# Gather, running sum and projection: fp32 gathers with a ScalarE cast in place of converting gathers, and some stores in two transfers

## The chip, the cores and the metric

The kernel runs on one core of a Trainium2 chip. The time is that of the device in microseconds (us), from the start of one execution to its end. The profile shows one such execution; its span goes from the first to the last instruction on the core and is a little shorter than the time. Engines are named as the profile does: PE is TensorE, DVE is VectorE, ACT is ScalarE, POOL is GpSimd, SP is SyncE. Besides them 16 DMA engines move data between HBM and the on-chip memory.

## What is computed

```python
B, S, N, D = 16, 4096, 2048, 512
# x: fp32 [B, S, D]; indices: int64 [B, N], ascending, without repeats; w: fp32 [D, D]
gathered = x[arange(B)[:, None], indices, :]
cs = cumsum(gathered, axis=1)
out = matmul(cs, w)          # fp32 [B, N, D]
```

For each of 16 batches 2048 rows of 512 numbers are gathered, a running sum is taken over them, and each summed row is multiplied by a 512 x 512 matrix. 67.1 MB are read by the gathers and 67.1 MB are written.

## The kernel before

The rows are cut into 256 tiles of 128 (16 a batch, `NT`), and two tiles make a pair (`R = 2`, 128 pairs). There is no scheduler: each engine has its own list of instructions, written out in order, and waits on semaphores. `Lane.need` puts a wait in only where the engine has not yet waited for as much. A tile passes through these steps:

- `gather(t)`, POOL, L112: an indirect DMA fetches 128 rows of `x`, one per partition. The destination `g16` is fp16 and the source fp32, so the DMA converts. There are `NG = 16` tile buffers (eight pairs); before POOL issues a gather it waits (`s_a`) until PE has summed the pair that was in the buffer.
- `sums(t)`, PE, L130: four matmuls with `g16` as the stationary operand and a triangle of ones (`ut`, or `uq` in the first and last pair) as the moving one. The result `pa` is the running sum within the tile, transposed: the 512 columns lie on the partitions in four blocks. There are four `pa` buffers.
- `carry(t)`, DVE, L162 (L149 at the start of a batch): adds the last column of the tile before and writes fp16 to `cst`. Four pair buffers.
- `project(u)`, PE, L173: four matmuls of 128x128 by 128x512, summed into one bank `pb`; four banks. The matrix `w` was converted to `w16` at the start (ACT at L319, DVE at L290).
- `drain(u)`, ACT, L185: copies `pb` to the fp32 output buffer `ob`, eight pair buffers. Before the first drain of a pair ACT waits until the store that last read that buffer has landed.
- `store(g)`, SP, L199: one DMA of 128 partitions by 1024 numbers (4 KB a partition) per pair, when both drains are done. The first and the last pair are stored tile by tile (L194), and their rows lie in plain order (`PLAIN`); in the others the triangle `ut` interleaves the rows so that each partition holds two neighbouring output rows.

PE's order is made ahead of time: sums run in front of projections by a lead that grows from 1 to `LEAD = 4` tiles over the first tiles and falls again over the last ones:

```python
lead = min(LEAD, 1 + u // 8, 1 + (T - 1 - u) // 6)
first = u if u // R in PLAIN else u // R * R + R - 1
while done < T and done <= max(first, u + lead):
```

DVE takes the carries in order of tiles, ACT the drains, SP the stores, POOL the gathers. Before the loop small DMAs bring indices and weights, and PE runs some matmuls on zeros (L269) until the first tile is there.

Of the kernel before, what the change touches and what calls it, by code (L numbers as in the profile page):

```python
# [7 lines left out]
P = 128  # L8
FP32 = mybir.dt.float32
FP16 = mybir.dt.float16  # L10
# [17 lines left out]
def kernel(  # L28
# [7 lines left out]
    nc = tc.nc  # L36

    B, S, D = x.shape
    N = indices.shape[1]
    R = 2  # L40
# [3 lines left out]
    T = B * NT  # L44
    G = T // R
# [2 lines left out]
    FIRST = 2 * R  # L48
    NG = 16
    LEAD = 4  # L50
    NA = 4
    NB = 4
    NC = 4
    NO = 8
    assert D == 512 and N % (R * P) == 0 and T % P == 0

    x_flat = x.rearrange("b s d -> (b s) d")

    const = ctx.enter_context(tc.tile_pool(name="const", bufs=1))
# [10 lines left out]
    ident = const.tile([P, P], FP32)  # L70
    zeros = const.tile([P, D], FP16)
    spare = const.tile([P, 1], FP16)
    g16 = [const.tile([P, R, D], FP16, name=f"g16_{i}") for i in range(NG // R)]
    cst = [const.tile([P, DC, R, P], FP16, name=f"cst{i}") for i in range(NC)]
    ob = [const.tile([P, R, D], FP32, name=f"ob{i}") for i in range(NO)]
    pa = [ps.tile([P, DC, R, Q], FP32, name=f"pa{i}") for i in range(NA)]
    pb = [ps.tile([P, D], FP32, name=f"pb{i}") for i in range(NB)]
# [3 lines left out]
    def sem(name):  # L81
        return tc.alloc_semaphore(name)

    s_z, s_ut, s_wc, s_if, s_pt, s_prep, s_of, s_c = (
        sem(f"s_{n}") for n in ("z", "ut", "wc", "if", "pt", "prep", "of", "c")
    )
# [5 lines left out]
    s_g = [sem(f"s_g{i}") for i in range(NG)]  # L92
    s_o = [sem(f"s_o{i}") for i in range(NO)]
    s_a = sem("s_a")
    s_d = sem("s_d")
    s_b = sem("s_b")
    s_e = sem("s_e")

    pool, pe, dve, act, sp = (
        Lane(e) for e in (nc.gpsimd, nc.tensor, nc.vector, nc.scalar, nc.sync)  # L100
    )

    def gather(t):
        g, r = divmod(t, R)
        pool.need(s_a, R * (g + 1) - NG)
        if t < FIRST:
            pool.need(s_first[g], 16)
            ap = idx_first[:, t, 0:1]
        else:
            pool.need(s_prep, t // P + 1)  # L110
            ap = idxg[:, t // P, t % P : t % P + 1]
        nc.gpsimd.indirect_dma_start(  # L112
            out=g16[g % (NG // R)][:, r, :],
            out_offset=None,
            in_=x_flat,
            in_offset=bass.IndirectOffsetOnAxis(ap=ap, axis=0),
            element_offset=(t // NT) * S * D,
        ).then_inc(s_g[t % NG], 16)


    PLAIN = (0, G - 1)

    def sums(t, u):
        g, r = divmod(t, R)
        pe.need(s_g[t % NG], 16 * (t // NG + 1))
        pe.need(s_d, t - NA + 1)
        for c in range(DC):
            if c == 1 and u is not None:
                pe.need(s_e, u - NB + 1)
            mm = nc.tensor.matmul(  # L130
                out=pa[t % NA][:, c],
                lhsT=g16[g % (NG // R)][:, r, c * P : (c + 1) * P],
                rhs=uq[:] if g in PLAIN else ut[:],
                start=(c == 0),
                stop=(c == DC - 1),
            )
        mm.then_inc(s_a, 1)

    def carry(t):
        g, r = divmod(t, R)  # L140
        dve.need(s_a, t + 1)
        src = pa[t % NA][:]
        if g in PLAIN:
# [22 lines left out]
    def project(u, t):  # L166
# [3 lines left out]
        for c in range(DC):  # L170
            if c == 2 and t is not None:
                pe.need(s_d, t - NA + 1)
            mm = nc.tensor.matmul(  # L173
# [8 lines left out]
    def drain(u):  # L182
        g, j = divmod(u, R)
        act.need(s_b, u + 1)
        nc.scalar.copy(out=ob[g % NO][:, j], in_=pb[u % NB][:]).then_inc(s_e, 1)  # L185

    def store(g):
        b, h = divmod(g, GB)
        rows = out[b, h * R * P : (h + 1) * R * P, :]
        if g in PLAIN:  # L190
            for j in range(R):
                sp.need(s_e, R * g + j + 1)
                done = s_ol[j] if g else (s_o[0], s_of)[j]
                nc.sync.dma_start(  # L194
                    out=rows[j * P : (j + 1) * P, :], in_=ob[g % NO][:, j]
                ).then_inc(done, 16)
            return
        sp.need(s_e, R * (g + 1))
        nc.sync.dma_start(  # L199
            out=rows.rearrange("(p j) d -> p j d", j=R), in_=ob[g % NO][:]  # L200
        ).then_inc(s_o[g % NO], 16)


    with nc.allow_non_contiguous_dma(reason="a few indices, one per partition"):
        for k, eng in enumerate((nc.sync, nc.scalar)):
            t = k * R
            eng.dma_start(  # L207
                out=idx_first[:, t : t + R, :],
                in_=indices[0, t * P : (t + R) * P]
# [7 lines left out]
    for k in range(KI):  # L217
        nc.sync.dma_start(
            out=idx64[:, k, :], in_=idx_rows[k * P : (k + 1) * P, :]
        ).then_inc(s_idx[k], 16)  # L220
    for g in range(G):
        store(g)
    for g in range(G - NO, G - 1):
        sp.need(s_o[g % NO], 16 * (g // NO + 1))
    for j in range(R):
        sp.need(s_ol[j], 16)

# [5 lines left out]
        out=ident[:],  # L233
        in_=ident[:],
# [7 lines left out]
        out=ut[:],  # L242
        in_=ut[:],
# [9 lines left out]
        out=uq[:],  # L253
        in_=uq[:],
# [6 lines left out]
    for t in range(T):  # L261
        gather(t)
# [15 lines left out]
    for k in range(KI):  # L278
# [3 lines left out]
            out=pb[k % NB][:, :P], in_=idxf[:, k, :], identity=ident[:]  # L282
# [16 lines left out]
    for u in range(T):  # L299
        lead = min(LEAD, 1 + u // 8, 1 + (T - 1 - u) // 6)  # L300
        first = u if u // R in PLAIN else u // R * R + R - 1
# [4 lines left out]
    for i, (is_sums, t) in enumerate(order):  # L306
        after = next((v for k, v in order[i + 1 :] if k != is_sums), None)
        if is_sums:
            sums(t, after)
        else:  # L310
            pe.need(s_wc, DC)
            project(t, after)
# [7 lines left out]
    for u in range(T):  # L320
        if u % R == 0:
            if u == R * NO:
                act.need(s_of, 16)
            act.need(s_o[u // R % NO], 16 * (u // R // NO))
        drain(u)


# [28 lines left out]
```

## Time and profile before

| | |
|---|---|
| time, median of 3 runs (lowest to highest) | 356.53 us (356.07 to 357.17) |
| the profiled execution: time, span | 356.07 us, 354.4 us |
| granted TensorE clock, mean | 0.993 |
| PE busy, share of the span | 310.2 us, 88% |
| ACT busy | 152.7 us, 43% |
| DVE busy | 179.0 us, 51% |
| POOL busy | 242.1 us, 68% |
| DMA packets, data moved (counted where it lands) | 57018, 102.35 MB |
| HBM read, written | 68.42 MB, 67.11 MB |
| gathers: time from issue to landing, median | 14.7 us |
| stores of a pair: issue to landing, median | 6.2 us |

Busy time is added up over all instructions of an engine; matmuls are pipelined, so a busy PE is not PE at its peak. The DMA digits of the slices are the mean busy share of the 16 DMA engines. Queue q0 carries POOL's gathers, q1 what SP issues (the stores above all). "POOL" in the chain that ended last is the issue of gathers, "DMA" the time from an issue to its landing where that is what the next step waited for.

### The profile page before, as it was taken

To read this page: it belongs to the slowest core of one execution; us is meant where nothing else is said; L and a number is where in the kernel's file an instruction comes from. 1 tells how busy PE (TensorE), PEld (TensorE's weight loads), DVE (VectorE), ACT (ScalarE), POOL (GpSimd) and SP (SyncE) were. 2 spreads that over 40 slices of the span, in tenths; PEclk is the share of its full clock that TensorE was granted. 3 is DMA by queue.
4 is the path that set the end of the run, shared out by engine and by line. 5 is a ranking of instruction groups with operands and counts; after the bars stand their busy time and mean duration, and the time that the engine had idled before them with its cause. 6 is when DMAs were issued, how large, how long until landed. Compare 5 with 4: busy or idle time off the path is not lost.

```text
span 354.4 us, 5499 instructions
## 1 busy us (share of the span) xinstructions
PE 310.2 (88%) x2071; PEld 148.7 (42%) x2071; DVE 179.0 (51%) x263; ACT 152.7 (43%) x260; POOL 242.1 (68%) x266
## 2 busy tenths in 40 slices
PE   5879899898899899898998898988988998889984
PEld 2345344344444444444444343444434444344432
DVE  1356555454555455455554555554555555455441
ACT  2135344444444444444444444444444444444542
POOL 6777777777777777777777777777767776776000
PEclk9899999999999999999999999999999999999998
DMA  7899999999999999999999999999999999999995
GB/s 192 122 235 276 307 280 307 296 296 310 292 302 307 289 312 296 295 305 298 303 303 294 302 300 296 298 306 293 304 302 302 302 294 302 306 290 304 310 322 204
DMA packets 57018, 102.35 MB, mean 289 GB/s; under 512 B 6816, under 2 KB 39840, under 8 KB 56992
## 3 DMA queue, kind: packets, MB, share of 16 engines
q0 software_dynamic: 36864, 33.57, 58.1%
q1 hardware_dynamic: 19568, 67.91, 50.8%
q10 hardware_dynamic: 560, 0.53, 0.4%
q8 instruction: 16, 0.26, 0.3%
q14 instruction: 10, 0.08, 0.1%
HBM read 68.42 MB, written 67.11 MB: 382 GB/s over the span
## 4 chain that ended last, share of the span: by engine, by line
DMA 62%; POOL 15%; PE 14%; issue 6%; DVE 1%; SPq 0%; ACT 0%
DMA g<-in_x_dram,idxg 61%; POOL g L112 15%; PE pb L173 8%; PE pa L130 4%; DMA idx<-in_indices_dram 1%; PE pb L269 1%; DVE cst L162 1%; SPq L216 0%; DVE cst L149 0%; PE pb L281 0%; ACT ob L185 0%; SPq L207 0%; DVE idxf L276 0%; SPq L351 0%; SPq L79 0%
## 5 line engine op out<-in xcount | busy, mean ns | idle before, releaser
L112 POOL DMA_INDIRECT g<-in_x_dram,idxg x252 | 236.7, 939 | 82.1 <-issue 57.8
L173 PE MATMUL pb<-w,cst 128*128 128x512 f16 x1024 | 262.5, 379 | 4.4 <-DVE cst L162 3.7
L162 DVE TENSOR_TENSOR cst<-pa,cst 128x512 f16<-128x512 f32 x240 | 166.0, 692 | 152.1 <-PE pa L130 151.6
L185 ACT COPY ob<-pb 128x512 f32<-128x512 f32 x256 | 150.1, 586 | 194.7 <-PE pb L173 194.7
L130 PE MATMUL pa<-ut,g 128*128 128x128 f16 x1008 | 98.5, 220 | 31.5 <-DMA g<-in_x_dram,idxg 29.1
L130 PEld LDWEIGHTS pa<-ut,g 128*128 128x128 f16 x1008 | 65.7, 98 | 124.1 <-DMA g<-in_x_dram,idxg 101.1
L173 PEld LDWEIGHTS pb<-w,cst 128*128 128x128 f16 x1024 | 89.2, 98 | 67.2 <-DVE cst L162 4.6
L149 DVE CAST cst<-pa 128x512 f16<-128x512 f32 x16 | 11.1, 692 | 10.6 <-PE pa L130 10.6
L269 PE MATMUL pb<-zeros 128*128 128x512 f16 x21 | 7.9, 549 | 1.5 <-DVE zeros L273 1.5
L269 PEld LDWEIGHTS pb<-zeros 128*128 128x128 f16 x21 | 2.8, 136 | 5.8 <-issue 4.1
L112 POOL DMA_INDIRECT g<-in_x_dram,idx_first x4 | 3.9, 987 | 1.6 <-issue 0.9
L276 DVE CAST idxf<-idx 128x128 f32<-128x128 uint32 x2 | 0.5, 228 | 5.7 <-DMA idx<-in_indices_dram 5.6
L281 PE MATMUL pb<-ident,idxf 128*128 128x128 f32 x2 | 0.7, 366 | 2.4 <-DVE idxf L276 2.4
L316 ACT ACT_TABLE_LOAD x1 | 1.3, 1283 | 2.5 <-issue 2.5
L281 PEld LDWEIGHTS pb<-ident,idxf 128*128 128x128 f32 x2 | 0.3, 139 | 3.0 <-issue 2.9
L319 ACT CAST w<-w 128x512 f16<-128x512 f32 x2 | 1.1, 614 | 0.7 <-DMA w<-in_w_dram 0.7
L130 PEld LDWEIGHTS pa<-uq,g 128*128 128x128 f16 x16 | 1.1, 98 | 0.7
L130 PE MATMUL pa<-uq,g 128*128 128x128 f16 x16 | 1.4, 219 | 0.0
L273 DVE MEMSET zeros<- 128x256 uint32 x1 | 0.3, 272 | 1.1 <-SPq L79 1.1
L290 DVE CAST w<-w 128x512 f16<-128x512 f32 x2 | 0.8, 418 | 0.0
L287 DVE CAST idxg<-pb 128x128 uint32<-128x128 f32 x2 | 0.6, 292 | 0.2 <-PE pb L281 0.2
L229 POOL MEMSET ident<- 128x128 f32 x1 | 0.2, 204 | 0.5 <-SPq L79 0.5
(10 smaller groups left out, 1.9 us busy)
## 6 DMA issues: line engine op xcount, KB each, us to landing
out_dram<-ob SPq DMA_DIRECT2D x126, 512.0 KB, 6.2
g<-in_x_dram,idxg POOLq DMA_INDIRECT x252, 14.7
out_dram<-ob SPq DMA_DIRECT2D x4, 256.0 KB, 2.2
w<-in_w_dram ACTq DMA_DIRECT2D x2, 256.0 KB, 4.1
w<-in_w_dram SPq DMA_DIRECT2D x2, 256.0 KB, 3.7
idx<-in_indices_dram SPq DMA_DIRECT2D x2, 128.0 KB, 4.4
g<-in_x_dram,idx_first POOLq DMA_INDIRECT x4, 4.0
idx_first<-in_indices_dram ACTq DMA_DIRECT2D x1, 2.0 KB, 2.1
```

Source lines behind the costliest of these rows:

```text
L112: nc.gpsimd.indirect_dma_start(out=g16[g % (NG // R)][:, r, :], out_offset=None, in_=x_flat, in_offset=bass.IndirectOffsetOnAxis(ap=ap, ax ...
L130: mm = nc.tensor.matmul(out=pa[t % NA][:, c], lhsT=g16[g % (NG // R)][:, r, c * P : (c + 1) * P], rhs=uq[:] if g in PLAIN else ut[:], star ...
L149: nc.vector.tensor_copy(out=dst, in_=src).then_inc(s_d, 1)
L162: nc.vector.tensor_tensor(out=dst, in0=src, in1=last, op=mybir.AluOpType.add).then_inc(s_d, 1)
L173: mm = nc.tensor.matmul(out=pb[u % NB][:], lhsT=cst[g % NC][:, c, j, :], rhs=w16[:, c, :], start=(c == 0), stop=(c == DC - 1),)
L185: nc.scalar.copy(out=ob[g % NO][:, j], in_=pb[u % NB][:]).then_inc(s_e, 1)
L269: nc.tensor.matmul(out=pb[NB - 1][:], lhsT=zeros[:, :P], rhs=zeros[:], start=True, stop=True)
L281: nc.tensor.transpose(out=pb[k % NB][:, :P], in_=idxf[:, k, :], identity=ident[:]).then_inc(s_pt, 1)
L287: nc.vector.tensor_copy(out=idxg[:, k, :], in_=pb[k % NB][:, :P]).then_inc(s_prep, 1)
L290: nc.vector.tensor_copy(out=w16[:, c, :], in_=w32[:, c, :]).then_inc(s_wc, 1)
L316: nc.scalar.copy(out=spare[:], in_=zeros[:, :1])
L319: nc.scalar.copy(out=w16[:, c, :], in_=w32[:, c, :]).then_inc(s_wc, 1)
```

## The change

The gathers land as fp32 in new buffers `g32` (again 16 tiles), and ACT converts them to fp16 in `g16`, which also has 16 tile buffers. `casts` fixes where ACT does it: before the drain of tile `u` all tiles up to `u + far` are cast, where `far` grows from 2 to `FAR = 10` over the first 64 tiles and falls to 2 at the end. While `far` is above 4 a whole pair is cast by one instruction, otherwise each tile by its own: 148 casts in all, 108 of them of pairs. A cast waits for the gathers of its tiles; the sums wait for the cast (`s_c`) where they waited for the gather, and POOL waits for the cast of the tile in the buffer where it waited for its sums.

Besides, the store of each 16th pair (the pairs 8, 24, ..., 120) is issued as two DMAs, one of the first 120 partitions and one of the last 8. The small one has its own semaphore `s_h`, for which ACT waits before the buffer is used again, and SP at the end. All other steps and PE's order are as before.

```diff
+    FAR = 10
+    NH = 8
...
+    CUT = 120
+    SPLIT = 16
...
-    g16 = [const.tile([P, R, D], FP16, name=f"g16_{i}") for i in range(NG // R)]
+    g32 = [const.tile([P, R, D], FP32, name=f"g32_{i}") for i in range(NG // R)]
+    g16 = [const.tile([P, R, D], FP16, name=f"g16_{i}") for i in range(NH)]
...
+    casts = []
+    cast_by = []
+    for u in range(T):
+        far = min(FAR, 2 + u // 8, 2 + (T - 1 - u) // 6)
+        casts.append([])
+        while len(cast_by) <= min(u + far, T - 1):
+            n = R if far > 4 and len(cast_by) % R == 0 else 1
+            casts[u].append((len(cast_by), n))
+            cast_by += [cast_by[-1] + 1 if cast_by else 1] * n
+
     def gather(t):
         g, r = divmod(t, R)
-        pool.need(s_a, R * (g + 1) - NG)
+        if t >= NG:
+            pool.need(s_c, cast_by[R * (g + 1) - NG - 1])
...
-            out=g16[g % (NG // R)][:, r, :],
+            out=g32[g % (NG // R)][:, r, :],
...
+    def cast(t, n):
+        g, r = divmod(t, R)
+        for u in range(t, t + n):
+            act.need(s_g[u % NG], 16 * (u // NG + 1))
+        nc.scalar.copy(
+            out=g16[g % NH][:, r : r + n], in_=g32[g % (NG // R)][:, r : r + n]
+        ).then_inc(s_c, 1)
+
     def sums(t, u):
-        pe.need(s_g[t % NG], 16 * (t // NG + 1))
+        pe.need(s_c, cast_by[t])
...
         sp.need(s_e, R * (g + 1))
-        nc.sync.dma_start(
-            out=rows.rearrange("(p j) d -> p j d", j=R), in_=ob[g % NO][:]
-        ).then_inc(s_o[g % NO], 16)
+        rows = rows.rearrange("(p j) d -> p j d", j=R)
+        cut = CUT if g % SPLIT == SPLIT // 2 else P
+        nc.sync.dma_start(out=rows[:cut], in_=ob[g % NO][:cut]).then_inc(s_o[g % NO], 16)
+        if cut < P:
+            nc.sync.dma_start(out=rows[cut:], in_=ob[g % NO][cut:]).then_inc(s_h, 16)
...
         if u % R == 0:
...
+            if (u // R - NO) % SPLIT == SPLIT // 2:
+                act.need(s_h, 16 * ((u // R - NO) // SPLIT + 1))
             act.need(s_o[u // R % NO], 16 * (u // R // NO))
+        for t, n in casts[u]:
+            cast(t, n)
         drain(u)
```

More of the change, by code (lines that the diff above doesn't have):

```diff
@@ L95 @@
     s_d = sem("s_d")
+    s_h = sem("s_h")
     s_b = sem("s_b")
@@ L131, in sums @@
                 out=pa[t % NA][:, c],
-                lhsT=g16[g % (NG // R)][:, r, c * P : (c + 1) * P],
+                lhsT=g16[g % NH][:, r, c * P : (c + 1) * P],
                 rhs=uq[:] if g in PLAIN else ut[:],
@@ L224 @@
         sp.need(s_o[g % NO], 16 * (g // NO + 1))
+    sp.need(s_h, 16 * (G // SPLIT))
     for j in range(R):
```

## The prediction

> **What bounds the kernel now.** The first view is the page's forty slices of the span, to see which resource is never idle.
>
> ```profile
> PE   5879899898899899898998898988988998889984
> ACT  2135344444444444444444444444444444444542
> POOL 6777777777777777777777777777767776776000
> DMA  7899999999999999999999999999999999999995
> ```
>
> PE and DMA are both near 9. PE's own work is short of the span: four projections of one tile take 0.86 us when nothing holds them (the chain's rows), and four sums of 128 columns a quarter of the columns, so about 1.08 us a tile, 276 us for 256 tiles. The chain that ended last says who holds it, first in shares, then row by row (start, length, what):
>
> ```profile
> DMA 62%; POOL 15%; PE 14%; issue 6%; DVE 1%; SPq 0%; ACT 0%
> ...
> 38.44 8.19 DMA g<-in_x_dram,idxg
> 116.79 11.94 DMA g<-in_x_dram,idxg
> 231.19 19.25 DMA g<-in_x_dram,idxg
> 320.75 20.59 DMA g<-in_x_dram,idxg
> ```
>
> A gather's time to land grows from 8 to 20 us. POOL issues one each 1.243 us (the chain's POOL rows: 84.45, 85.70, 86.94) and the transfers fall behind it. The same is in the table by stretch for tile g (PE busy with its matmul count, PEld, POOL with its issues, clock, DMA share, GB/s):
>
> ```profile
> 60.00:80.00 20.00, 6.17 (x64) 4.03 (x64) 15.11 (x17) 1.00 1.14 298
> 160.00:180.00 20.00, 5.96 (x62) 4.04 (x63) 15.03 (x17) 1.00 1.14 299
> 260.00:280.00 20.00, 5.91 (x60) 3.79 (x60) 14.34 (x16) 1.00 1.14 300
> ```
>
> About 61.5 matmuls, four a tile, in 20 us: one tile in 1.30 us, the same everywhere, with the DMA share at 1.14. So the DMA engines are full from about 30 us to the end, and POOL waits only when the 16 gather buffers are all in flight. That shows in the waits (total, times, longest):
>
> ```profile
> ACT ob L185 <- PE pb L173: 194.7, 256, 8.5
> PEld pa L130 <- DMA g<-in_x_dram,idxg: 101.1, 155, 1.2
> POOL g L112 <- PE pa L130: 24.0, 62, 0.8
> ```
>
> The queues tell what fills the engines (packets, MB, time of their packets as a share of 16 engines):
>
> ```profile
> q0 software_dynamic: 36864, 33.57, 58.1%
> q1 hardware_dynamic: 19568, 67.91, 50.8%
> ```
>
> Together 108.9%: packets overlap, so their durations can't be added; the distance between starts is needed. The trace has one record per packet (queue, start, duration, size), and I counted the commonest start-to-start distances between 40 and 320 us. A converting gather row lasts 96 ns, the next gather row starts 79 ns after it, a store packet 78 ns after it. A 4 KB store packet lasts 172 ns there and the gather row behind it starts after 168 ns; at the end, with the gathers over, stores last 159 to 160 ns and follow each other after 155. Each engine has 8 gather rows and 4 store packets a tile, one from each queue in turn while both have some: 4 x (78 + 168) + 4 x 79 = 1300 ns. That is the 1.30 us of the table, so this sum is the model.
>
> **The change, part by part.** *Gathers land as fp32 (g32).* The plain 2 KB row is in the trace: the weight loads' packets last 84 ns and start 80 ns apart. Of a store, the 13 ns between 168 and 155 appear only behind converting rows; its duration grows by the same 12 to 13 ns by which a converting row (96) outlasts a plain one (84). I read it as the converter's delay, uncovered at each change from store to gather. Without it: 4 x 155 + 8 x 80 = 1260 ns, 40 ns a tile less. About 246 tiles land in the full stage: -9.8 us. Bounds: no mixing of plain rows and stores is in this trace, so the 168 may stay (1312, +3.0 us with rows at 80) or the rows may go at the bytes' own pace, 75 ns (75 ns more for 2 KB more, 159 less 84: 4 x 155 + 8 x 75 = 1220, -19.7, less what POOL then limits). I take 155 and 80, both measured on plain packets.
>
> The Trainium skill, "DMA: Bandwidth & Descriptors", section "Bandwidth", speaks against this part: it prices traffic by bytes through 16 ports, 435 GB/s, and gives conversion no price; both kernels read the same 134 MB, estimate 308 us, so by that page this term would be zero and the forecast 358.5. The 1300 ns a tile against 155 and 80 on plain packets is why I don't follow it.
>
> *POOL.* Same 256 issues, 0.937 us and 0.306 us of issue each. Without waits the last begins at 8.4 + 251 x 1.243 = 320.4 us (326.0 now), lands some 4 to 13 us later, before 335. So POOL is just under the new DMA rate (1.243 against 1.260); if the issue of plain rows costs otherwise, each 10 ns above 1.260 is 2.5 us. I take the same. The buffer is freed by the cast instead of the sums: nothing, as 16 tiles are 20 us and a landing should be 8 to 13.
>
> *ACT casts.* 108 of pairs and 40 of single tiles. A 128x512 fp32 to fp16 cast is 614 ns (L319), a copy of one element 193 (L316), so 1024 elements are 614 + 421 = 1035 ns. In all 108 x 1.035 + 40 x 0.614 = 136 us, ACT 153 to 289 us. Per pair: 2 x 586 (L185) + 1035 = 2207 ns against 2520 of DMA: hidden, with 313 ns to spare. Casts wait for gathers in ACT's order; behind each stand two drains, and behind those PE (four pb banks) and SP's stores. That is covered as the casts run 10 tiles ahead of the drains and the sums at most 4 or 5: PE has five cast tiles in hand. If that cover is gone, what ACT needs above 2520 is paid 128 times. At the ends a single cast is on the path: +0.6 before the first store, +0.6 after the last landing.
>
> *Longer lag of stores.* Drains are 10 tiles behind the casts, where now they are about 5 behind the sums. Five tiles of stores, 5 x 0.62 = 3.1 us of DMA time, move from the first 85 us towards the end. Nothing if the DMA queue never runs dry, 3.1 if all of it was idle: in that build-up 640 + 8/9 x 620 = 1191 ns of work come per 1243 ns of POOL. The engines that end last have the deepest queue; I take +0.8.
>
> *Split stores.* Eight stores as 120 and 8 partitions; eight more SP issues of 332 ns on a queue that waits 288 us: nothing. The Trainium skill ("DMA: Bandwidth & Descriptors", section "Why a DMA increments its semaphore by 16 and not by 1") has the engine count as the largest divisor up to 16 of the partitions, 15 and 8, the lowest-numbered; no run here shows which engine a packet took. By the packets: if one engine is left out, it saves 8 x 8 x 155 ns = 9.9 us, and others get up to 8 x 155 = 1.2 us more. The 16 completion marks of late gathers spread over 7.5 us, the last 2.4 behind the middle. So from -2.4 to +1.2; I take 0. The wait for s_h on ACT comes eight pairs (20 us) after a store that lands in 6.2: nothing.
>
> Sum: -9.8 + 0.6 + 0.6 + 0.8 = -7.8 us. The profiled execution took 356.07 us, 1.67 more than its span of 354.4; so 348.3, and as the median of the runs lies 0.46 above it, 348.7. With the bounds of split, lag and row pace this case is 344 to 353.
>
> **Rivals.** *The change of queue itself costs the 13 ns (slower).* Then a store costs 168 beside plain rows too: 1312 ns a tile, +3.0, with 0.6 + 0.6 + 0.8: +5.0, 361.5; with rows at 79 and no lag +2.2, 358.7. For it: both rows of the 168 are mixed traffic. Against: the store's duration grows by just the converter's 12. It decides above 168 - (2.0/0.246 + 8)/4 = 164 ns from store to gather.
>
> *POOL becomes the bound (faster still).* If mixed plain rows take 75 to 78 ns, a tile is under 1243; the last gather lands at 320.4 + 5, and with the 8.2 us now between last landing (346.2) and end, plus a cast, the span is 335 to 340: 339 us. For it: the bytes' pace; against it the 80 between plain loads.
>
> *ACT becomes the bound.* If a cast or its waits add 400 ns a pair, ACT needs 2607: 128 x 87 ns = 11 us back, 360. Against: two casts in a row at L319 took 1.14 us together, less than twice 614.
>
> **How the numbers follow.** The forecast 0.62, the queue rival 0.20, POOL 0.10, ACT 0.08. About 0.3% (1.1 us) is what a measurement of this kernel can tell from no change. Faster: nearly all of the forecast and POOL, 0.70; same: 0.07, the edge of the forecast and of the queue rival with rows at 79; slower: 0.23. The range takes the forecast whole, half of POOL's case and the mild half of the others: 342.5 to 358.5.
>
> **What would show it.** Right: the median gather packet at 84 ns instead of 96, store packets near 159, store to gather 155; a tile each 1.26 us in the same table; landings of 5 to 13 us that hardly grow; POOL's waits for buffers near none; ACT near 290 us busy with idle left. Wrong: store packets still 172, or ACT without gaps and DMA slices below 9, or landings that again climb to 20.

## The result, and the profile after

The changed kernel takes 352.57 us (median of four runs, 352.15 to 352.7), the kernel before 356.65 us beside it (356.07 to 357.17): a ratio of 0.9884, with a 95% interval of 0.9866 to 0.9902. That is 4.1 us faster, where 7.8 were forecast. (Here and below the medians are over all runs, while the ratios leave out runs more than 1.5% above the fastest of their kernel.) The profiled execution took 352.7 us, its span 350.8 us, at a granted clock of 0.993. On three other chips the sign was the opposite; that stands with the experiments.

First the slices of the span, on the page of the changed kernel:

```profile
PE   5878877999898989998989889989989899988984
ACT  3368876877787778787878678777877788877883
POOL 6777777777777777777777777777777777776000
DMA  7799999999999999999999999999999999999974
```

PE and DMA look as before; ACT has risen from 4 to 7 or 8 and keeps gaps. The DMA row now drops in its last two slices, while PE and ACT are still at work: the end belongs less to the transfers. The queues (packets, MB, time of their packets as a share of 16 engines) show what the packets became:

```profile
q0 software_dynamic: 20480, 67.13, 49.5%
q1 hardware_dynamic: 19624, 67.91, 48.2%
```

Queue q0 has 16384 packets fewer, at twice the bytes: two plain rows of 2 KB go as one packet of 4096 bytes, where each converting row was a packet of its own. The two pages' rows for q1 price the stores: (50.8% of 354.4 less 48.2% of 350.8) x 16 / 16384 = 10.7 ns less for each of the 16384 store packets. In the records a store now lasts 159 ns at the median (172 before) and so does a pair of rows. Counted as in the prediction, a store and the pair of rows behind it start 155 or 156 ns apart most often, with smaller groups up to 163; the 168 of before is gone.

The chain that ended last, shares and then rows (start, length, what):

```profile
POOL 39%; DMA 20%; issue 15%; PE 13%; ACT 10%; DVE 1%; SPq 0%; ACTq 0%
...
79.79 7.60 DMA g<-in_x_dram,idxg
...
177.31 9.86 DMA g<-in_x_dram,idxg
...
232.32 12.37 DMA g<-in_x_dram,idxg
...
299.84 15.40 DMA g<-in_x_dram,idxg
```

DMA had 62% of this chain and POOL 15%. Now POOL's issues come first, 1.251 us apart, yet the time for a gather to land still grows. The stretches for tile g (PE, PEld, ACT, POOL busy with counts, clock, DMA share, GB/s):

```profile
60.00:80.00 20.00, 6.62 (x68) 4.90 (x68) 9.20 (x9) 15.12 (x17) 1.00 1.03 404
160.00:180.00 20.00, 7.26 (x63) 4.60 (x64) 8.30 (x8) 15.13 (x17) 1.00 1.03 413
260.00:280.00 20.00, 7.19 (x62) 4.47 (x63) 8.37 (x8) 15.12 (x17) 1.00 1.03 414
```

The DMA share, packet durations over engine time, fell from 1.14 to 1.03, and 300 GB/s became 413, for a tile that now carries 524288 bytes (gather and store) in place of 393216. At 413 GB/s a tile is 1.269 us; at 300 it was 1.31.

The mean hides a spread. Each gather gives 16 completion marks, one for each share of it. I read from the trace how they advance over 160 tiles from about the 60th on, and when those of the last gather came:

| us | before | after |
|---|---|---|
| middle mark, per tile | 1.314 | 1.252 |
| last mark, per tile | 1.317 | 1.288 |
| last gather: its issue begins | 325.95 | 322.34 |
| its middle mark | 344.2 | 331.5 |
| its second last mark | 346.0 | 333.6 |
| its last mark | 346.2 | 339.5 |

Before, all sixteen fell behind POOL together. After, the middle goes at POOL's pace, 62 ns a tile better, and one of the sixteen shares falls behind the rest, 2 us at the 112th tile and 8 us at the 232nd. A cast needs all sixteen, so the kernel gained only the 29 ns of the slowest. The profile does not name the engine of a mark. The Trainium skill, "DMA: Bandwidth & Descriptors", section "Latency and other measured facts", calls two of the sixteen engines usually slower than the others; the one late share is in that direction, but no run here shows which engine it was.

The waits (total, times, longest):

```profile
ACT g L144 <- DMA g<-in_x_dram,idxg: 53.2, 92, 1.3
PEld pa L155 <- ACT ob L210: 46.9, 79, 1.7
PEld pa L155 <- ACT g L144: 30.4, 50, 1.3
ACT ob L210 <- PE pb L198: 23.1, 32, 4.1
POOL g L129 <- ACT g L144: 6.4, 21, 0.3
```

ACT waits 53.2 us for gathers, so ACT does not set the pace; POOL's waits for buffers fell from 24.0 to 6.4 us. The sums' wait for the drain (L210) is one that the kernel before hardly has: the second of the four matmuls of `sums` waits for `s_e`, the drain that frees the bank `pb` of the projection behind it. All of the 46.9 us lie in front of that second matmul. Casts stand before the drains in ACT's order, so drains come later than before; whether this costs time is seen below, with the shorter lead.

Last, the tail of the timeline, ACT's rows (start, length; in brackets the idle time before, and what ended it):

```profile
339.57 0.59 ACT L210 COPY ob<-pb 128x512 f32<-128x512 f32 x1 [0.50 <-PE pb L198]
...
340.05 0.62 ACT L144 CAST g<-g 128x512 f16<-128x512 f32 x1
340.60 0.59 ACT L210 COPY ob<-pb 128x512 f32<-128x512 f32 x1
...
341.08 0.62 ACT L144 CAST g<-g 128x512 f16<-128x512 f32 x1
...
342.98 0.59 ACT L210 COPY ob<-pb 128x512 f32<-128x512 f32 x1 [1.28 <-PE pb L198]
...
343.46 0.62 ACT L144 CAST g<-g 128x512 f16<-128x512 f32 x1
```

The gather of the last tile landed at 339.5 and its cast began at 343.46, 4.0 us later. In ACT's order it stands behind two more casts, three drains, and the 1.28 us in which the third of these waited for PE, which itself had waited for a cast. From the last landing to the end of the span it is 11.3 us, where it was 8.2.

### The profile page after: what moved, and what is told of

Its sections match the earlier page's. It is cut to its first block, busy times and chain, and to the rows that moved or that the text cites. A ratio compares the mean times of both kernels' runs of the same rounds, so it can differ in the third digit from the quotient of the medians.

```text
span 350.8 us, 5683 instructions
## 1 busy us (share of the span) xinstructions
PE 306.8 (87%) x2071; PEld 153.8 (44%) x2071; DVE 179.0 (51%) x263; ACT 264.5 (75%) x408; POOL 243.9 (70%) x266
## 3 DMA queue, kind: packets, MB, share of 16 engines
q1 hardware_dynamic: 19624, 67.91, 48.2%
## 4 chain that ended last, share of the span: by engine, by line
POOL 39%; DMA 20%; issue 15%; PE 13%; ACT 10%; DVE 1%; SPq 0%; ACTq 0%
POOL g L129 39%; DMA g<-in_x_dram,idxg 19%; PE pb L198 8%; ACT g L144 7%; ACT ob L210 3%; PE pa L155 3%; DMA idx<-in_indices_dram 1%; PE pb L297 1%; DVE cst L187 1%; SPq L243 0%; DVE cst L174 0%; PE pb L309 0%; SPq L234 0%; ACTq L23 0%; DVE idxf L304 0%
## 5 line engine op out<-in xcount | busy, mean ns | idle before, releaser
L144 ACT CAST g<-g 128x1024 f16<-128x1024 f32 (+1 forms) x148 | 137.6, 931 | 56.2 <-DMA g<-in_x_dram,idxg 53.2
L210 ACT COPY ob<-pb 128x512 f32<-128x512 f32 x256 | 139.9, 585 | 23.3 <-PE pb L198 23.1
L155 PE MATMUL pa<-ut,g 128*128 128x128 f16 x1008 | 110.7, 220 | 31.8 <-ACT ob L210 21.0
L155 PEld LDWEIGHTS pa<-ut,g 128*128 128x128 f16 x1008 | 70.9, 98 | 115.8 <-ACT ob L210 46.9
```

The lines of the kernel that those rows point to most:

```text
L144: nc.scalar.copy(out=g16[g % NH][:, r : r + n], in_=g32[g % (NG // R)][:, r : r + n]).then_inc(s_c, 1)
L155: mm = nc.tensor.matmul(out=pa[t % NA][:, c], lhsT=g16[g % NH][:, r, c * P : (c + 1) * P], rhs=uq[:] if g in PLAIN else ut[:], start=(c == 0),
```

## Experiments

I held the forecast's theory, that conversion in the DMA delayed the stores behind it, against two rivals: that the split stores made the gain, and that the new step on ACT limits it. On three of the four chips that the experiments ran on, PE's results reached the other engines late and the kernel before took 404 to 412 us, so the runs there tell of packets and of that condition, not of the 352.57 us. By the profile a carry on DVE began there 1.4 to 2.6 us (medians of the runs without split stores and with the split alone) after the tile's sums had ended, where it is 0.04 us in the two kernels at 353 and 356 us. The traces of those chips also hold fewer semaphore events (3875 and 2952 in these two runs, 7936 and 7695 in the other two), so what released a wait is less sure in them.

**Changed kernel without split stores.**

```diff
-    CUT = 120
+    CUT = P
-    sp.need(s_h, 16 * (G // SPLIT))
-            if (u // R - NO) % SPLIT == SPLIT // 2:
-                act.need(s_h, 16 * ((u // R - NO) // SPLIT + 1))
```

> The changed kernel with every store whole (no 120 + 8). In the changed kernel's trace one of the 16 completion marks of a gather falls behind the others, 8 us behind the middle at the end, the other 15 stay together. If the engine that the 120-partition stores leave out is that slow one, its lag here grows by the 9.9 us it was spared (8 stores x 8 packets x 155 ns), limited by the 16 buffers, and the time rises by 3 to 8 us, to 356 to 360. If the split does nothing for the slow engine, the lag stays at 7 to 8 us and the time at 352 to 353; if the small transfers are what slows it (1.2 us each on eight engines), the time falls by about 1 us.

Measured: 445.81 us beside 406.03 of the kernel before, ratio 1.091 (1.0854 to 1.0967). Again on another chip:

> The changed kernel with every store whole, once more: in the first try the kernel before took 406 us beside it, with TensorE's granted clock at 0.93 and its results reaching the other engines late, so the DMA was not what set the pace there. Where the kernel before takes 356 to 357: if the engine that the 120-partition stores leave out is the slow one of the changed kernel, its lag behind the middle grows from 8 towards 16 us and the time is 354 to 358; if not, lag 7 to 8 us and 352 to 353.

Measured: 451.81 beside 409.84, 1.1012 (1.0935 to 1.1088).

**Twice as many splits** (each eighth pair).

```diff
-    SPLIT = 16
+    SPLIT = 8
```

> The changed kernel with each 8th store split in place of each 16th: 16 split stores. If the engine left out is the slow one, its lag shrinks from 8 us to about none and the time falls by 1 to 4 us (349 to 351), then another engine or the work after the last landing sets the end. If it is another engine, the lag stays or grows by the second 1.2 us of the small transfers and the time is 352 to 354.

Measured: 445.7, ratio 1.0947 (1.0909 to 1.0986).

**The split alone**, in the kernel before: its `store` becomes that of the changed kernel, with the waits for `s_h`, and nothing else.

```diff
+    CUT = 120
+    SPLIT = 16
...
+        cut = CUT if g % SPLIT == SPLIT // 2 else P
+        nc.sync.dma_start(out=rows[:cut], in_=ob[g % NO][:cut]).then_inc(s_o[g % NO], 16)
+        if cut < P:
+            nc.sync.dma_start(out=rows[cut:], in_=ob[g % NO][cut:]).then_inc(s_h, 16)
```

> The kernel before, with converting gathers, and only the stores split. Theory that the converter's delay in the DMA engines is what the change took away: same time within 1 us or up to 1.5 us faster (355 to 357), a tile still each 1.30 us, as all 16 engines are full there. Rival that the split brought the gain: 352 to 353.

Measured: 405.49 beside 406.03, ratio 0.9989 (0.996 to 1.0018).

**Converting gathers and the copy on ACT**: everything changed but the conversion; the cast becomes a copy from fp16 to fp16.

```diff
-    g32 = [const.tile([P, R, D], FP32, name=f"g32_{i}") for i in range(NG // R)]
+    g32 = [const.tile([P, R, D], FP16, name=f"g32_{i}") for i in range(NG // R)]
```

> The changed kernel with g32 held as fp16: the gathers convert in the DMA again and ScalarE copies fp16 to fp16, all waits, buffers, leads and split stores as in the changed kernel. Theory of the converter's delay: packets of 96 ns and stores of 172 ns return, a tile each 1.29 to 1.30 us, and with the two casts at the ends and the longer tail the time is 356 to 360, slower than before. Rival that the deeper buffering or the split brought the gain: 352 to 353, as the changed kernel.

Measured: 447.45, ratio 1.0962 (1.0906 to 1.1017). Again on another chip:

> The changed kernel with g32 as fp16 (the DMA converts, ScalarE copies fp16 to fp16), once more, beside a kernel before at 356 to 357. Theory of the converter's delay: gather rows of 96 ns in packets of 1 KB, stores of 172 ns, a tile each 1.29 to 1.30 us, 356 to 360 us. Rival that the buffering or the split brought the gain: 352 to 353 us.

Measured: 451.53, ratio 1.0971 (1.0871 to 1.107).

**The changed kernel, unaltered, on such a chip.**

> The changed kernel as it is, beside the kernel before on this chip. Where the kernel before takes 356 us: 352 to 353, ratio 0.988. Where it takes 404 to 410 and TensorE's results come late: ratio 1.09 to 1.10, as the three others with casts on ScalarE, since there the drains wait for TensorE and hold the casts behind them in ScalarE's order; 1.00 or less would say that the casts in that order are not what costs there.

Measured: 445.85 beside 405.67, ratio 1.0962 (1.0914 to 1.101).

What follows from these seven. On these chips the split gains nothing: alone it changed nothing, and with none, 8 or 16 of them the intervals overlap. And whatever has the cast on ACT costs 9 to 10% there, converting or not: 451.53 and 451.81 us on one chip. So transfers are not the limit there. The chain's shares by engine, of the split alone and then of the changed kernel without split stores on the same chip, from their pages:

```profile
PE 76%; issue 13%; another core or an unknown queue 3%; DVE 3%; ACT 2%; DMA 1%; SPq 0%; ACTq 0%; DVEq 0%
```

```profile
PE 66%; another core or an unknown queue 9%; ACT 9%; issue 9%; DVE 5%; DMA 1%; SPq 0%; ACTq 0%; DVEq 0%
```

DMA has 1% in both. With the casts ACT's share grows from 2% to 9%, and the waits of that second run point the same way:

```profile
POOL g L129 <- ACT g L144: 96.4, 37, 6.2
ACT ob L210 <- PE pb L198: 87.1, 73, 3.4
```

Drains wait for late PE results, the casts behind them in ACT's order wait too, and POOL waits 96.4 us for the casts, against 6.4. That this order is what costs the 9% is argued, not shown: the run meant to tell it (casts behind drains, below) came on a chip where PE was not late. The granted clock was lower with the casts too (0.893 against 0.931), but PE's busy time grew by only 9.5 us, from 325.8 to 335.3, of a span that grew by 40.

What these runs do show is the effect of conversion on the packets by itself, since two on one chip differ in it and in the split only. Queues, first of the kernel that converts and copies (span 449.9), then of the changed kernel without splits (449.4), both from the second chip:

```profile
q0 software_dynamic: 36864, 33.57, 52.8%
q1 hardware_dynamic: 19624, 67.91, 39.9%
```

```profile
q0 software_dynamic: 20480, 67.13, 47.3%
q1 hardware_dynamic: 19568, 67.91, 37.9%
```

With the same order on every engine, the converting one again has rows of 96 to 98 ns one by one, and 168 ns from a store to the gather behind it; without conversion rows go in pairs of 159 ns. The stores cost (39.9% of 449.9 less 37.9% of 449.4) x 16 / 16384 = 9.0 ns more a packet with conversion. That is less than 10.7, and the median store lasts 162 ns, not the 172 that was expected; the engines are not always full there, so fewer stores have a gather row next to them (an inference, not counted). The conversion, not the new schedule, makes the difference in the packets.

**Transfers alone.** Gathers and stores of the kernel before with the sums, carries, projections and drains left out: a store sends a constant from `ob` once its pair's gathers have landed and the store eight pairs before it is done, and POOL waits only for the landing in the same buffer. Once converting, once to fp32, once to fp32 with the split stores.

```diff
-        pool.need(s_a, R * (g + 1) - NG)
+        pool.need(s_g[t % NG], 16 * (t // NG))
...
+        for t in range(R * g, R * g + R):
+            sp.need(s_g[t % NG], 16 * (t // NG + 1))
+        sp.need(s_o[g % NO], 16 * (g // NO))
...
-    g16 = [const.tile([P, R, D], FP16, name=f"g16_{i}") for i in range(NG // R)]
+    g16 = [const.tile([P, R, D], FP32, name=f"g32_{i}") for i in range(NG // R)]
...
-    CUT = P
+    CUT = 120
```

The first two parts of the diff, and what is left out, are in all three, the third in the second and third, the last in the third.

> Only the transfers of the kernel before: the 256 converting gathers and the 128 stores, with the sums, projections, drains and casts left out; a store waits for its pair's gathers to land and sends a constant, POOL waits for the landing in the same buffer. So the DMA engines are measured without TensorE. Theory of the converter's delay: a tile each 4 x (78 + 168) + 4 x 79 = 1300 ns, landings that grow to 20 us, about 340 to 347 us. Rival, conversion costs the engines nothing: the same time as the plain one, within 2 us.

> The same with plain fp32 gathers, whole stores. Theory: 155 to 158 ns per 4 KB packet, 8 a tile, 1250 to 1265 ns, which is about POOL's 1250: landings of 5 to 10 us, and 8 to 11 us less than the converting one, 332 to 338. Rival, conversion costs nothing: within 2 us of the converting one. Besides, of the slow engine: the fetches of instructions (16 of 16 KB, 1 us each in the changed kernel) hardly occur here; if they all burden one engine, no completion mark falls 8 us behind here; if that engine is slow in itself, it does.

> The same with plain gathers and each 16th store as 120 and 8 partitions. If the engine left out is the one that ends last, its lag is less than with whole stores and the time up to 5 us less; if not, the same time within 1 us.

Measured, two runs each: 366.56, 365.47 and 370.42 us. By time that is a miss for the theory and what its rival had (within 2 us): without conversion only 1.1 us are gained, and the split, expected to gain up to 5 us or to change nothing, costs 4.9. The stretches show where it went. Converting, then plain (PE, PEld, DVE, ACT at zero, POOL, clock, DMA share, GB/s):

```profile
60.00:100.00 40.00, 0.00 (x0) 0.00 (x0) 0.00 (x0) 0.00 (x0) 30.20 (x33) 0.50 1.13 299
100.00:150.00 50.00, 0.00 (x0) 0.00 (x0) 0.00 (x0) 0.00 (x0) 37.80 (x41) 0.50 1.14 298
250.00:300.00 50.00, 0.00 (x0) 0.00 (x0) 0.00 (x0) 0.00 (x0) 39.05 (x36) 0.50 1.13 292
```

```profile
60.00:100.00 40.00, 0.00 (x0) 0.00 (x0) 0.00 (x0) 0.00 (x0) 30.26 (x32) 0.50 1.03 417
100.00:150.00 50.00, 0.00 (x0) 0.00 (x0) 0.00 (x0) 0.00 (x0) 37.84 (x40) 0.50 1.03 410
250.00:300.00 50.00, 0.00 (x0) 0.00 (x0) 0.00 (x0) 0.00 (x0) 39.05 (x37) 0.50 1.01 373
```

Between 60 and 100 us a tile takes 393216 bytes / 299 GB/s = 1.315 us converting and 524288 / 417 = 1.257 us plain: 58 ns a tile. Between 100 and 150 us it is 393216 / 298 = 1.320 against 524288 / 410 = 1.279: 41 ns. No other engine's work explains that. It is the theory's mechanism by itself, and its size is about the 40 ns of the forecast; the middle marks of the whole kernel gained 62. Later POOL's issues stretch in both, to 1.40 us apart (the issue itself from 0.94 to 1.10 us) and without a wait, and the last gather packet ends at 339 us in both. Then 24 us of stores follow, at a DMA share of 0.45 to 0.49, about half of what full engines show. Why POOL slows there, and why the stores that are left keep only half of the engines' time busy, stays open. In the whole kernel POOL's issues stay 1.251 us apart to the end and ACT paces the last stores, so these totals say little of it. What was expected of the late share could not be read here: the second of these traces holds 450 of the 4096 completion marks.

**Casts behind the drains.** ACT drains first and casts afterwards, one tile further ahead at both ends.

```diff
-        far = min(FAR, 2 + u // 8, 2 + (T - 1 - u) // 6)
+        far = min(FAR, 3 + u // 8, 3 + (T - 1 - u) // 6)
...
+        if u:
+            drain(u)
         for t, n in casts[u]:
             cast(t, n)
-        drain(u)
+        if not u:
+            drain(u)
```

> The changed kernel with ScalarE's order turned: the casts due at a tile come behind its drain, one tile further ahead so that the sums still find them. Nothing else is changed. Theory: what the changed kernel loses where TensorE's results come late is that a cast of 1.05 us, or its wait for a gather, stands in front of a drain that frees a pb bank; with the drain in front the bank is free up to 1 us earlier. Where the kernel before takes 404 to 412 us: ratio 1.02 to 1.06 in place of 1.096; where it takes 356 to 357: 350 to 353 us. Rival: it is the mere work of ScalarE, or casts that wait behind late drains, so that the order does not matter: 1.09 to 1.10.

Measured, on a chip where the kernel before took 356.31: 355.0 us, ratio 0.9981 (0.9955 to 1.0007). The 350 to 353 us expected for such a chip were missed. It is slower than the changed kernel: the last gather lands at 341.7 us (339.5 there), and the tail behind it is 11.2 us, not shorter (11.3). This order does not help.

**A shorter lead of the casts.**

```diff
-    FAR = 10
+    FAR = 6
```

> The changed kernel with casts at most 6 tiles in front of the drains in place of 10. If the lead only delays stores (the +0.8 us of the forecast) and has no use where TensorE's results come late: ratio within 0.01 of the changed kernel's 1.096. If the lead is what covers late results (a cast behind a late drain delays the sums): 1.11 or more. Where the kernel before takes 356 to 357: 350 to 353 us, as the stores come 5 us earlier.

Measured beside the same 356.31: 353.11 us, 0.1 us above what was expected; ratio 0.9906 (0.9888 to 0.9923), which overlaps the changed kernel's interval. The last landing is at 338.9 and the tail 12.4 us; the order of the last 24 tiles is the same in both, as `far` is 6 or less there. The waits of the sums' weight loads for casts trebled, from 30.4 to

```profile
PEld pa L155 <- ACT g L144: 92.3, 131, 1.5
```

while their 46.9 us of waits for drains are gone, and the time hardly moved: in the middle PE has the slack, and neither these waits nor the length of the lead is what bounds this kernel. Again the last of the 16 marks fell behind, by 8.3 us over the last 16 tiles (median; 8.1 in the changed kernel, 9.6 with casts behind drains), so a late share is not a chance of one run. Whether the split stores ease that share on a chip where PE is not late was not tried. If they leave one engine out, they save it 9.9 us by the forecast's sum, more than the 6.75 us by which the last landing came earlier; so how much of those 6.75 us is the split's is open. The 62 ns a tile of the middle mark cannot come from one engine spared. No version was faster than the changed kernel.

## Why the prediction was right in sign and mechanism, and too large

The forecast was faster by 7.8 us through the converter's delay, and the measured 352.57 lies in its range, 3.9 us above its number. Point by point:

**The converter's delay: right.** Stores at 159 ns and mixed packets that start mostly 155 ns apart are the values that were taken; the transfers alone gave 41 to 58 ns a tile and the chain lost two thirds of its DMA share. The Trainium skill's pricing by bytes ("DMA: Bandwidth & Descriptors", section "Bandwidth"), by which this term would be zero, does not agree with the 1.315 against 1.257 us that the transfers alone took to read the same 524288 bytes a tile (399 against 417 GB/s read). Once conversion is gone, 417 is 96% of that page's 435 GB/s.

**Its size: the first term, -9.8 us, measured -6.75** at the last landing (346.22 to 339.47; what the split stores have in it is open). The step that failed is "Each engine has 8 gather rows and 4 store packets a tile", read as sixteen equal engines at 1260 ns. The mean was near it (1.269 us a tile by 413 GB/s). The middle share of the gathers went faster, 1.252 us, which is POOL's pace: a pair of rows replaces two rows at 80, and 4 x 155 for stores and 4 x 155 for pairs are 1240. One share went at 1.288. The forecast had seen 16 marks spread over 7.5 us with the last 2.4 behind, and used them only for the split; as long as all were late together that spread cost nothing.

**POOL: nearly right, and it mattered less.** An issue took 1.251 us in place of 1.243, from 946 ns where 939 were; the last came at 322.3, not 320.4. POOL paces the middle share, as the rival "POOL becomes the bound" had it, and its rows of "75 to 78 ns" were the better value. Its 339 us failed because the last share landed 17.1 us after the issue, not 5, and for the tail.

**ACT: right that it is hidden.** A pair's cast took 1.05 us (1.035 forecast). ACT was busy 264.5 us, not 289: the groups of L144 and L210 add to 137.6 + 139.9 = 277.5, as neighbouring instructions overlap. It kept 53.2 us of waits for gathers. "That is covered" was not quite so: PE's weight loads waited 46.9 us for drains that came later behind the casts, but the run with the shorter lead, which has none of these waits, took the same time.

**The last cast: +0.6 forecast, +3.1 measured** (8.2 to 11.3 us between last landing and end). The cast's own 0.62 us was counted, not its place in ACT's order: "+0.6 after the last landing" left out the two casts, three drains and the wait for PE that stand before it. That is the second mis-sized term.

**Lag of stores, +0.8: not seen.** With the lead cut from 10 to 6 tiles nothing was gained. **Split stores, 0:** so it was in the kernel before on a chip with PE late; in the transfers alone they cost 4.9 us; in the changed kernel on the chip of the result it is open.

The sum by measured terms: -6.75 at the last landing, which holds the start's +0.6, and +3.1 behind it make -3.6, from a span of 354.4 to 350.8. Against the forecast's 346.6 that is 4.2 more, 2.5 of it in the tail and 1.7 at the last landing (337.8 by the forecast's terms: 346.2 - 9.8 + 0.6 + 0.8).

**The rival by the change of queue** (361.5) fell with the 155 to 163 ns and the 41 to 58 ns a tile. **ACT as the bound** (360) did not come about on the chips where the kernel before takes 356 us. On those where PE's results came late, ACT's share of the chain grew and the change made the kernel 9 to 10% slower. No row of the one trace before could show that.

## What to carry to other kernels

A cast in the DMA can cost more than its own packets show: look at what a packet of the other queue costs next to converting rows, and price the two by the distance of their starts. A transfer is done when its slowest share is, so before summing by mean rates read how the completion marks spread, and expect the spread to matter, as it did here, once the transfers as a whole no longer fall behind. A step that is hidden in the middle is on the path at the end, with everything that stands before it in its engine's order.

## What the runs showed of the hardware that was not expected

Plain gather rows of 2 KB went two to a packet, 16384 packets of 4096 bytes for 32768 rows, and cost the same as a store packet, 159 ns; converting rows went singly. With plain gathers one of the 16 shares of the transfers fell 8 us behind the middle one in 350 us, with converting gathers 2 to 3. And the same kernel took 356 us on some chips and 404 to 412 on others, with PE's results late and a granted clock of 0.87 to 0.94; the ranking of the two kernels turns round between them, 0.9884 against 1.0962, and the cause of that state was not found.
